# The third block solve of a chunked DeltaNet between the steps of its scan, and all gate blocks in the scan

## The chip, the cores and the metric

The kernel runs on one core of a Trainium2 chip. The metric is the device time of one execution in microseconds (us), from several runs of the same program; one more execution was recorded by the hardware profiler and is the source of every row below. The engines are TensorE (PE, its weight loads PEld), VectorE (DVE), ScalarE (ACT), GpSimd (POOL) and SP, whose queue issues nearly all DMAs.

## The reference, cut to what matters

One layer of a diffusion block over 512 latent tokens (and 256 context tokens that only feed the recurrent states), width 1024. Three mixers run on one input projection; their outputs are weighted by gates. This change touches the first mixer, a gated DeltaNet in chunks of 64 tokens, 8 heads of 128, in both directions, and the gates' projections.

```python
m = jnp.where(strict, jnp.einsum('bhnid,bhnjd->bhnij', kb, k) * decay, 0.0)
t_inv = lax.linalg.triangular_solve(eye + m, jnp.broadcast_to(eye, m.shape), left_side=True, lower=True)
u = jnp.einsum('bhnij,bhnjd->bhnid', t_inv, v * beta[..., None])
w = jnp.einsum('bhnij,bhnjd->bhnid', t_inv, kb * jnp.exp(gc)[..., None])
...
def step(state, inp):
    q_i, k_i, u_i, w_i, a_i, d_i = inp
    v_new = u_i - jnp.einsum('bhcd,bhde->bhce', w_i, state)
    o_i = jnp.einsum('bhcd,bhde->bhce', q_i, state) + jnp.einsum('bhcs,bhse->bhce', a_i, v_new)
    state = state * d_i[..., None, None] + jnp.einsum('bhcd,bhce->bhde', k_i, v_new)
    return state, o_i
...
o = rms_norm(o, norm_g) * jax.nn.silu(z)
...
g_dn, g_hy, g_lru = jnp.split(jax.nn.sigmoid(p_gate), N_BRANCH, axis=-1)
merged = g_dn * (o_dn @ w_proj_dn) + g_hy * (o_hy @ w_proj_hy) + g_lru * (o_lru @ w_proj_lru)
```

Each of the 12 chunks and 2 directions needs the inverse of a 64x64 unit triangular matrix per head before its step of the scan; the two directions run through the chunks in opposite order within the context (4 chunks) and the latent tokens (8 chunks).

## The kernel before, in words

All large products run in three passes on split weights and inputs (`mm3`: high x high, high x low, low x high). `load_w` loads a weight block of 512 KB into one of three raw buffers `wr`, splits it into one of two high (`wh`) and two low buffers (`wl`); the engines of the split are given per call (`e_hi`, `e_lo`). A gate block (`gate`, or `gate_halves` in two halves) is one `load_w`, 24 matmuls of 512 columns, one activation on ScalarE (L574) and one store to `gated` (L575). There are 24 such blocks beside the eight done early (`fill`: three kinds, eight each).

The inverses come from three solves (`solve`), two with four tiles of one direction each (`solve_first(0)`, `solve_first(1)`, on `M1`), and a third with the remaining two tiles of both directions (`solve_second`, on `M3`). A solve works on 32x32 blocks: transposes on VectorE bring the blocks' rows side by side (L819), 31 pairs of VectorE instructions eliminate column by column (L827, L829), transposes bring the inverse back (L837, L839), and TensorE makes the off-diagonal block from two chains of small products (L853, L857) with copies on ScalarE (L854, L858). The result is stored to `wad`, from where the scan loads it as `wa`. `solve` is a generator; `run` draws from the generators round by round and puts one piece of other work (`each`) behind every third round (`EVERY`). Before, 12 pieces (six values, six gates) lie beside the first two solves, and the remaining values and six gates beside the third (`NW1`, `NFILL`). A value (`value`, `value_out`) is a projection of 48 matmuls, a convolution of six VectorE instructions (L485 to L487), an activation and transposes.

The scan (`step`, L976 to L1041) has 12 steps. In each, both directions advance by a chunk: `chunk_loads` loads `v`, `kd` (three buffers each) and `wa` (ring `war`, four buffers); from step 1 on GpSimd scales the queries and keys by the decay (L992, L994); TensorE multiplies by the state (L1005); VectorE subtracts (L1009); TensorE applies the inverse (L1015); ScalarE copies the result (L1017). After the first `yield`, TensorE makes the state's increment (L1023), VectorE updates the state in 16 instructions (L1028; ScalarE instead in step 0, L1030), and in steps 4 to 11 TensorE finishes the output (L1035). Each step has two gaps, one at each `yield`; before, one half of a gate stands in each of the 24 gaps. Behind eight of the steps four `mod_part`s follow (a 512 KB load into a `wr` buffer and one VectorE instruction, L1052 or L1054), and before every third step a `mod_sum` (a few TensorE instructions into the bank of the gates).

Instructions are ordered per engine when the program is built: an instruction is placed when the scheduler's model has it ready, those written earlier first. In the scan, TensorE's order is fixed to the written one (`in_order((ET.PE,))`); the other engines' is not.

## Time and profile before

| | us |
|---|---|
| median of 3 runs | 1676.78 |
| lowest, highest | 1674.07, 1689.07 |
| profiled execution | 1676.85 |
| its span, first to last instruction | 1675.1 |
| TensorE busy | 1529.7 (91%) |
| VectorE busy | 1195.7 (71%) |
| ScalarE busy | 615.7 (37%) |
| GpSimd busy | 589.3 (35%) |

The busy times are from the page's first part. A matmul's recorded end is modelled, so matmuls overlap in the records and a busy TensorE need not be one at its peak; starts tell more than durations. The granted clock is a share of the upper level (2.4 GHz); at 0.5 it is the lower one. DVE, ACT and POOL instructions are recorded from start to end. SPq is SP's queue: what it "waited for" is what the next DMA in its order had to wait for.

### The profile page before, as it was taken

Reading aid. Unit: us, or ns where it says so; the run is one execution under the profiler, and the core shown is the slowest. Engines: PE = TensorE matmul, PEld = TensorE weight load, DVE = VectorE, ACT = ScalarE, POOL = GpSimd, SP = SyncE. Lnnn points to the kernel's source line nnn. Section 1 sums busy time; section 2 is a strip of 40 time slices with the busy share of each in tenths; the row PEclk is TensorE's granted clock in tenths of the full one; section 3 lists DMA queues with packets and bytes.
Section 4 is the critical chain, followed back from the end, with each engine's and each line's share of the span. In section 5 each row is a group of like instructions: output and inputs, shape, how many; then the busy total and the mean of one; then the engine's idle time right before and its main releaser. Section 6 shows DMA issues by size and latency. Waiting matters only on the chain. (4 is left out here: it accounts for less than half of the span.)

```text
span 1675.1 us, 23659 instructions
## 1 busy us (share of the span) xinstructions
PE 1529.7 (91%) x9176; PEld 1258.0 (75%) x9176; DVE 1195.7 (71%) x1752; ACT 615.7 (37%) x1011; POOL 589.3 (35%) x401
## 2 busy tenths in 40 slices
PE   6899888889999899887999889999999999999998
PEld 2677777767887777775788678787888788888876
DVE  6877888756656997834666375777766899989873
ACT  4367787734553232320111330333222433333311
POOL 4653534325444360312434114222321233334441
PEclk9899999999999896878899999999999999999999
DMA  9432222335344332577888736322462223232331
GB/s 343 162 107 82 76 76 81 103 104 175 127 126 125 110 101 74 173 211 206 233 227 244 253 109 231 107 88 84 162 207 64 68 96 97 92 101 98 104 113 50
DMA packets 93056, 225.66 MB, mean 135 GB/s; under 512 B 9963, under 2 KB 30699, under 8 KB 92176
## 3 DMA queue, kind: packets, MB, share of 16 engines
q1 hardware_dynamic: 92112, 217.86, 41.6%
q0 software_dynamic: 832, 6.29, 0.9%
q8 instruction: 72, 1.18, 0.3%
q14 instruction: 40, 0.33, 0.1%
HBM read 190.45 MB, written 33.66 MB: 134 GB/s over the span
## 5 line engine op out<-in xcount | busy, mean ns | idle before, releaser
L173 PE MATMUL bank<-region,region 128*128 128x512 f32 (+1 forms) x2032 | 761.8, 376 | 28.9 <-DVE region L487 6.8
L175 PE MATMUL bank<-region,region 128*128 128x512 f32 (+1 forms) x2032 | 755.2, 373 | 25.1 <-DVE region L160 22.1
L174 PE MATMUL bank<-region,region 128*128 128x512 f32 (+1 forms) x2032 | 757.2, 373 | 4.2 <-DVE region L160 2.1
L173 PEld LDWEIGHTS bank<-region,region 128*128 128x128 f32 x2032 | 389.7, 192 | 106.8 <-ACT region L155 10.4
L175 PEld LDWEIGHTS bank<-region,region 128*128 128x128 f32 x2032 | 389.5, 192 | 98.6 <-DVE region L160 28.6
L174 PEld LDWEIGHTS bank<-region,region 128*128 128x128 f32 x2032 | 390.6, 192 | 69.0 <-DVE region L418 4.4
L160 DVE TENSOR_TENSOR region<-region,region 128x1024 fp32r<-128x1024 f32 (+2 forms) x241 | 268.7, 1128 | 174.1 <-ACT region L155 98.2
L155 ACT ACTIVATE region<-region 128x1024 fp32r<-128x1024 f32 (+2 forms) x209 | 178.4, 865 | 422.9 <-PE bank L174 132.8
L160 POOL TENSOR_TENSOR region<-region,region 128x1024 fp32r<-128x1024 f32 (+1 forms) x64 | 157.3, 2463 | 237.9 <-ACT region L155 200.4
L157 POOL TENSOR_SCALAR region<-region 128x1024 fp32r<-128x1024 f32 (+1 forms) x96 | 114.3, 1193 | 330.4 <-PE bank L174 147.7
L1423 DVE SCALAR_TENSOR_TENSOR region<-bank,pc,region 128x441 f32<-128x441 f32 (+2 forms) x352 | 224.8, 688 | 4.3 <-ACT region L1412 0.7
L485 DVE SCALAR_TENSOR_TENSOR region<-bank,pc,region 128x511 f32<-128x511 f32 (+1 forms) x56 | 34.1, 629 | 48.7 <-ACT region L482 45.8
L1054 DVE SCALAR_TENSOR_TENSOR region<-region,cc,region 128x1024 f32<-128x1024 f32 x28 | 41.7, 1488 | 33.9 <-DMA region<-in_w_mod_dram 33.4
L992 POOL TENSOR_TENSOR region<-region,region 128x512 f32<-128x512 f32 x32 | 49.1, 1564 | 39.5 <-DMA region<-rowd 36.8
L482 ACT ACTIVATE region<-bank,pc 128x512 f32<-128x512 f32 (+1 forms) x40 | 23.1, 597 | 98.6 <-PE bank L175 98.6
L1435 POOL TENSOR_TENSOR region<-region,region 128x512 f32<-128x512 f32 x22 | 34.3, 1561 | 66.3 <-DVE region L1423 52.3
L1028 DVE SCALAR_TENSOR_TENSOR region<-region,egl,bank 128x128 f32<-128x128 f32 x160 | 42.3, 339 | 21.3 <-PE bank L1023 21.3
L1005 PE MATMUL bank<-region,region 128*64 128x128 f32 x608 | 42.4, 306 | 9.2 <-DVE region L1028 9.2
L1005 PEld LDWEIGHTS bank<-region,region 128*64 128x64 f32 x608 | 39.8, 157 | 14.4 <-DVE region L1028 6.4
L1017 ACT ACTIVATE region<-bank 128x512 f32<-128x512 f32 x24 | 14.3, 598 | 89.9 <-PE bank L1015 89.9
L574 ACT ACTIVATE region<-bank 128x512 f32<-128x512 f32 x32 | 18.8, 588 | 70.6 <-PE bank L175 66.4
L1137 POOL TENSOR_TENSOR region<-region,region 128x512 f32<-128x512 f32 x8 | 12.2, 1523 | 85.6 <-DVE region L1121 85.6
(275 smaller groups left out, 1669.7 us busy)
## 6 DMA issues: line engine op xcount, KB each, us to landing
region<-in_w_in_dram SPq DMA_DIRECT2D x97, 512.0 KB, 3.9
region<-in_w_mod_dram SPq DMA_DIRECT2D x48, 512.0 KB, 6.2
region<-in_ffn_up_dram SPq DMA_DIRECT2D x44, 512.0 KB, 3.5
region<-in_w_proj_dram SPq DMA_DIRECT2D x24, 512.0 KB, 3.6
region<-in_ffn_down_dram SPq DMA_DIRECT2D x22, 512.0 KB, 3.5
gated<-region SPq DMA_DIRECT2D x32, 256.0 KB, 2.1
region<-gated SPq DMA_DIRECT2D x32, 256.0 KB, 4.0
kdd<-region SPq DMA_DIRECT2D x16, 384.0 KB, 2.8
```

What stands on the lines that cost most here:

```text
L155: act(hi, raw, AF.Copy)
L157: nc.gpsimd.tensor_scalar(hi, raw, 1.0, 0.0, op0=ALU.mult, op1=ALU.add)
L160: (vtt if e_lo == "dve" else gtt)(lo, raw, hi.bitcast(F32), op=ALU.subtract)
L173: mmul(ps, lh, rh, start=start, stop=False)
L174: mmul(ps, lh, rl, start=False, stop=False)
L175: mmul(ps, ll, rh, start=False, stop=stop)
L992: gtt(wq[d][:, hs], KQ[hf][:, :, chs[d] - 4], eg[:, hs].unsqueeze(2).to_broadcast([P, 4, 2, 64]), op=ALU.mult)
L1005: mmul(X[hf][rcs[d], h, :], wq[d][:, hf * 4 + h, kind], S[d][:, hf * 4 + h, :], start=(kind == 0 or h == 0), stop=(kind == 0))
L1028: stt(S[d][:, h], S[d][:, h], egl[:, d, c, i, h:h + 1], p3[hf][d][:, h % 4], op0=ALU.mult, op1=ALU.add)
L1054: stt(acc, w_, cc[:, k, 0:1], acc, op0=ALU.mult, op1=ALU.add)
L1423: stt(uv[:, ro, co], pv_[:, ri, ci], w[:, a * 3 + b:a * 3 + b + 1], uv[:, ro, co], op0=ALU.mult, op1=ALU.add)
L1435: gtt(uu[0], uu[0], uu[1], op=ALU.mult)
```

## The change

The third solve leaves its own stage. Beside the first two solves lie the eight values alone (`NFILL = 0`), and no gate. All 24 gate blocks lie in the scan, 48 halves in 24 gaps, so two halves in each. `solve_second` is started ahead of the scan (`next(later)`: its opening transposes) and then advanced at every gap, four pieces in steps 0 to 3 and one from step 4 on; its block products get a `yield` between the forward and the back half. It uses buffers at 68, 72, 64 and 65 instead of 180 to 190, and banks 6 and 7. The scan's `wa` ring has two buffers in steps 0 to 6 (92 and 96) and four from step 7 on; `M3` (at 100) is in use until its store. Gate stores in the scan are issued by ScalarE's queue instead of SP's; `mod_sum` has bank 1 of its own. The six gates that were split on ScalarE and GpSimd (`"act", "pool"`) beside each solve now use the default engines, GpSimd for the high and VectorE for the low part.

```diff
--- before.py
+++ after.py
@@ -569,10 +569,10 @@
     def load_gate(z_, m, e_hi="pool", e_lo="dve"):
         return load_w(I["w_in"][GATES[z_][0] + m], e_hi=e_hi, e_lo=e_lo)
 
-    def gate_store(z_, m, pg):
+    def gate_store(z_, m, pg, store=load):
         th = ur([P, NL])
         act(th, pg, GATES[z_][1])
-        load(gated[z_, m], th)
+        store(gated[z_, m], th)
 
     def gate(z_, m, e_hi="pool", e_lo="dve"):
         w = load_gate(z_, m, e_hi, e_lo)
@@ -598,7 +598,7 @@
     ksr, knr, kdr = ring(3, [143, 140]), ring(3, seq(146, 3, 2)), ring(3, seq(152, 3, 2))
     qsr, jkr = ring(2, seq(140, 2, 5)), ring(0.5, seq(158, 0.5, 4))
     atr = ring(1, [170, 171])
-    NFILL = 12
+    NFILL = 0
 
     dcw = pv("dn_conv_w").rearrange("p (b j) -> p b j", j=4)
     kdd = dr.tile([2, TT, P, NH, P], F32, name="kdd")
@@ -843,15 +843,19 @@
         for half in range(2):
             zp = dn([P, 16, 32])
             rp = dn([P, 16, 32])
+            blocks = []
             for c in range(2):
                 d = dirs[c]
                 pj = slice(c * 64 + d * 32, c * 64 + d * 32 + 32)
                 pi = slice(c * 64 + (1 - d) * 32, c * 64 + (1 - d) * 32 + 32)
                 ci = slice((1 - d) * 32, (1 - d) * 32 + 32)
+                blocks.append((pj, pi, ci))
                 for a in range(16):
                     e = half * 16 + a
                     mmul(zp[pi, a, :], M[pj, e, ci], Wu[pj, e, :], start=True, stop=True)
                 act(Z[pi, half * 512:half * 512 + 512], zp[pi].rearrange("p a b -> p (a b)"), AF.Copy)
+            yield
+            for pj, pi, ci in blocks:
                 for a in range(16):
                     e = half * 16 + a
                     mmul(rp[pj, a, :], Z[pi, e * 32:e * 32 + 32], M[pi, e, ci], start=True, stop=True)
@@ -867,7 +871,7 @@
 
     def solve_second():
         yield from solve((0, 1), M3.rearrange("p t c h i -> p (t c h) i"),
-                         [at(180 + 4 * i, [P, 32, 32]) for i in range(2)], ring(1, seq(188, 1, 2)), "dve")
+                         [at(68 + 4 * i, [P, 32, 32]) for i in range(2)], ring(1, seq(64, 1, 2)), "dve")
         for d in range(2):
             for t, i in enumerate(second[d]):
                 load(wad[d, i, :, 0, :].rearrange("(c j) x -> j c x", c=2),
@@ -922,7 +926,7 @@
                 each.pop(0)()
 
     fill = [(z_, m) for z_ in range(3) for m in range(8)]
-    EVERY, NW1 = 3, 12
+    EVERY = 3
     vss = {}
 
     def values_(h):
@@ -933,10 +937,7 @@
 
     values = [lambda h=h: values_(h) for h in range(9)]
     ur = ring(2, [152, 154])
-    gates = [lambda f=f: gate(*f, "act", "pool") for f in fill[:NFILL]]
-    work = [w_ for p_ in zip(values, gates) for w_ in p_] + values[len(gates):] + gates[len(values):]
-    run([solve_first(0), solve_first(1)], work[:NW1])
-    run([solve_second()], work[NW1:])
+    run([solve_first(0), solve_first(1)], values + [lambda f=f: gate(*f, "act", "pool") for f in fill[:NFILL]])
     for nm, x_ in (("kdd", kdd), ("vd", vd), ("rowd", rowd)):
         dump(nm, x_)
     dump("egl", egl)
@@ -952,10 +953,11 @@
 
 
     ur = ring(2, [186, 188])
-    mm = Banks([0])
+    dn = Banks([6, 7])
+    mm, mm1 = Banks([0]), Banks([1])
     o = at(60, [P, 4, NH, P])
     S = [at(84 + 4 * d, [P, NH, P]) for d in range(2)]
-    war = ring(4, seq(92, 4, 4))
+    wars = [ring(4, [92, 96]), ring(4, [100, 104, 92, 96])]
     kdr, vr = ring(4, seq(140, 4, 3)), ring(4, seq(152, 4, 3))
     wqr = ring(4, seq(164, 4, 3))
     egr = ring(2, seq(176, 2, 2))
@@ -964,7 +966,7 @@
 
     def chunk_loads(s, lat):
 
-        v, kd, wa = vr([P, NH, P]), kdr([P, NH, P]), war([P, 2 if lat else 1, NH, 64])
+        v, kd, wa = vr([P, NH, P]), kdr([P, NH, P]), wars[s >= 7]([P, 2 if lat else 1, NH, 64])
         for d in range(2):
             i, c = divmod(order[d][s], 2)
             rc = slice(c * 64, c * 64 + 64)
@@ -1055,7 +1057,7 @@
 
     def mod_sum(q):
         if q in (1, 2):
-            mp = mm([P, 8])
+            mp = mm1([P, 8])
             for b in range(8):
                 mmul(mp[:, b:b + 1], acc[:, b * P:(b + 1) * P], ones[:, 0:1], start=True, stop=True)
             vtt(mod34[:, q - 1], mp, pv("b_mod")[:, 16 + q * 8:24 + q * 8], op=ALU.add)
@@ -1063,7 +1065,7 @@
             row, brow = wr([1, D]), wr([1, D])
             load(brow, I["b_mod"][:, (2 + q) * D:(3 + q) * D])
             for b in range(2):
-                mp = mm([1, 512])
+                mp = mm1([1, 512])
                 mmul(mp, ones[:, 0:1], acc[:, b * 512:(b + 1) * 512], start=True, stop=True)
                 vtt(row[:, b * 512:(b + 1) * 512], mp, brow[:, b * 512:(b + 1) * 512], op=ALU.add)
             load(modr[0 if q == 0 else 1].unsqueeze(0), row)
@@ -1073,10 +1075,12 @@
         project_part(w, [(pg, hh, hl)], 0, 4)
         yield
         project_part(w, [(pg, hh, hl)], 4, 8)
-        gate_store(z_, m, pg)
+        gate_store(z_, m, pg, nc.scalar.dma_start)
         yield
 
     first_ins = len(bb.instructions)
+    later = solve_second()
+    next(later)
     halves = (None for z_, m in fill[NFILL:] for _ in gate_halves(z_, m))
     ngap, FBM = 2 * (24 - NFILL), 1
     gap = 0
@@ -1088,9 +1092,11 @@
             gap += 1
             for _ in range(gap * ngap // 24 - (gap - 1) * ngap // 24):
                 next(halves)
+            for _ in range(4 if s_ < 4 else 1):
+                next(later, None)
         for k in range(4) if s_ % 3 < 2 else ():
             mod_part(s_ // 3, s_ % 3 * 4 + k)
-    assert next(halves, 1) == 1
+    assert next(halves, 1) == 1 and next(later, 1) == 1
     in_order((ET.PE,))
     dump("o", o)
     if upto <= 3:
```

## Rows read from the trace of the kernel before

**Rows 1.** Busy time by stretch; stretch: length, busy us per engine, granted clock, DMA share, GB/s
```profile
540.00:671.00 131.00, 117.40 (x956) 98.55 (x951) 116.29 (x221) 36.53 (x58) 43.23 (x13) 0.85 0.30 97
671.00:743.35 72.35, 60.98 (x484) 52.18 (x483) 43.18 (x57) 21.37 (x33) 21.14 (x14) 0.83 0.65 191
743.35:809.00 65.65, 52.76 (x452) 41.65 (x452) 34.80 (x62) 8.71 (x16) 14.79 (x13) 0.87 0.75 209
809.00:950.30 141.30, 132.77 (x1475) 112.61 (x1476) 82.07 (x174) 19.46 (x34) 51.97 (x37) 0.95 0.84 232
```

**Rows 2.** Timeline of TensorE: start, us, instruction, [idle before it and its releaser]
```profile
743.35 0.66 PE L1015 MATMUL bank<-region,region 64*64 64x128 f32 x2 [5.51 <-DMA region<-vd]
...
955.01 0.79 PE L173 MATMUL bank<-region,region 128*128 128x512 f32 x1 [4.24 <-ACT region L155]
```

**Rows 3.** SP's waits, 738 to 950 us: us in total, times, longest
```profile
SPq L575 <- ACT region L574: 35.1, 8, 9.0
```

**Rows 4.** Timeline of VectorE, first stage
```profile
592.21 1.12 DVE L485 SCALAR_TENSOR_TENSOR region<-bank,pc,region 128x511 f32<-128x511 f32 x2
...
595.36 1.79 DVE L827 TENSOR_TENSOR region<-region,region 128x256 f32<-128x256 f32 x1
...
647.63 1.88 DVE L839 STREAM_TRANSPOSE region<-region 32x1024 f32<-32x1024 f32 x1
```

**Rows 5.** Groups by line, 540 to 720 us: count, busy us, mean ns, idle before
```profile
L827 DVE TENSOR_TENSOR region<-region,region 128x31 f32<-128x31 f32 (+15 forms) x93 | 35.5, 406 | 1.1
L829 DVE TENSOR_TENSOR region<-region,region 128x31 f32<-128x31 f32 (+15 forms) x93 | 31.8, 365 | 1.1
L819 DVE STREAM_TRANSPOSE region<-region 32x1024 f32<-32x1024 f32 x12 | 25.5, 2121 | 0.3
L837 DVE STREAM_TRANSPOSE region<-region 32x1024 f32<-32x1024 f32 x12 | 25.4, 2118 | 0.3
...
L858 ACT ACTIVATE region<-bank 32x512 f32<-32x512 f32 x8 | 4.7, 588 | 18.8 <-PE bank L857 18.8
```

**Rows 6.** Timeline of all engines, from 683 us
```profile
683.07 2.39 POOL L160 TENSOR_TENSOR region<-region,region 128x1024 fp32r<-128x1024 f32 x1 [1.18 <-ACT region L155]
683.12 2.62 DVE L827 TENSOR_TENSOR region<-region,region 128x252 f32<-128x252 f32 x1
```

**Rows 7.** Timeline of TensorE, block products and gate matmuls
```profile
625.64 1.19 PE L853 MATMUL bank<-region,region 32*32 32x32 f32 x32 [1.16 <-DVE region L839]
...
691.18 0.40 PE L174 MATMUL bank<-region,region 128*128 128x512 f32 x1
...
695.95 0.39 PE L174 MATMUL bank<-region,region 128*128 128x512 f32 x1
```

**Rows 8.** DMA issues, 640 to 738 us: count, KB each, median us to landing
```profile
wad<-region SPq DMA_DIRECT2D x11, 256.0 KB, 2.9
...
region<-wad SPq DMA_DIRECT2D x4, 128.0 KB, 5.1
```

**Rows 9.** One line's instructions: count, ns min/median/max, first and last start
```profile
L575 SPq DMA_DIRECT2D gated<-region x32: 319/327/531, 125.5 to 955.5; - x32
```

**Rows 10.** Groups by line, 743 to 951 us
```profile
L1028 DVE SCALAR_TENSOR_TENSOR region<-region,egl,bank 128x128 f32<-128x128 f32 x160 | 42.3, 339 | 21.3 <-PE bank L1023 21.3
...
L1054 DVE SCALAR_TENSOR_TENSOR region<-region,cc,region 128x1024 f32<-128x1024 f32 x25 | 37.8, 1512 | 29.3 <-DMA region<-in_w_mod_dram 28.9
...
L1009 DVE TENSOR_TENSOR region<-region,bank 128x512 f32<-128x512 f32 x22 | 14.7, 681 | 5.8 <-PE bank L1005 5.8
...
L160 DVE TENSOR_TENSOR region<-region,region 128x1024 fp32r<-128x1024 f32 x10 | 13.8, 1378 | 23.5 <-POOL region L157 23.5
...
L157 POOL TENSOR_SCALAR region<-region 128x1024 fp32r<-128x1024 f32 x10 | 11.3, 1134 | 85.2 <-DMA region<-wad 30.3 <-PE bank L174 18.6 <-DMA region<-kdd 13.1
...
L994 POOL TENSOR_TENSOR region<-region,region 128x256 f32<-128x256 f32 x6 | 5.2, 887 | 14.5 <-PE bank L1005 14.3
```

**Rows 11.** DMA issues, 738 to 950 us
```profile
region<-kdd SPq DMA_DIRECT2D x20, 256.0 KB, 8.6
```

## The prediction

> **What bounds the kernel now.** I first cut the span with the busy-time-by-stretch view around the code that moves [rows 1]. The four stretches are the first two solves with their values and gates (540.00 to 671.00), the third solve with the last values and gates (to 743.35), the scan's steps 0 to 3 (to 809.00) and steps 4 to 11 (to 950.30). TensorE is the busiest engine in all four, yet never full: it lacks 13.6, 11.4, 12.9 and 8.5 us, and the granted clock is 0.85, 0.83, 0.87 and 0.95 of the upper level, so part of its busy time is stretched. VectorE has 116.3 of 131 us in the first stretch and 53 to 60% in the other three. So the first stretch is a VectorE stretch, steps 4 to 11 are a TensorE stretch, and the two in between are neither: something waits there. The timeline of TensorE shows what for: the scan's first matmul stood 5.51 us for the load of `vd`, and the first projection after the scan 4.24 us for a weight split on ScalarE [rows 2]. The list of waits on SP adds that SP, whose queue carries every load, stood 35.1 us in the scan at L575, the gate store, for ScalarE, once for 9.0 us [rows 3]; every load behind it starts later.
>
> **The change part by part.** I work on one clock, that of the profiled execution: 1675.1 us of span, 1676.85 us of time, 0.07 from the median 1676.78. A shift of the scan's end is taken as a shift of that time.
>
> *The first stage.* It keeps two solves and gets all eight values; six gates leave it. VectorE's last transpose of the first two solves begins at 647.63 and lasts 1.88, so it ends at 649.5 [rows 4]. What changes before that: the third solve's four opening transposes, done early, leave (4 x 2.121 = 8.5) [rows 5]. Two values come in, each with six convolution instructions: the solve is interrupted from 592.21 to 595.36 for one value [rows 4], so 6.3. And VectorE meets fewer splits on GpSimd. One such meeting reads: GpSimd's split starts at 683.07 and takes 2.39, the solve's instruction started at 683.12 takes 2.62 [rows 6], where the mean is 0.406 [rows 5]. Six gates less and two values more are four splits less, worth 0 to 4 x 2.2 = 8.8; I take 2, since most splits fall beside convolutions. The end moves to 649.5 - 8.5 + 6.3 - 2 = 645.3. TensorE has fewer matmuls here than now, so I cost them at nothing; VectorE covers them.
>
> *From there to the scan.* The last block products: two groups forward, two back, 1.19 each at the full clock [rows 7], with four copies of 0.588 [rows 5], 7.1; I take 8.5. Then SP stores (2.9 to landing) and loads `wad` (5.1) [rows 8], with two issues 8.9. The first scan matmul comes at 645.3 + 8.5 + 8.9 = 662.7 instead of 743.35: -80.7. Bounds: all of the 8.8 and 7.1 give 654.5; the products as slow as now (the stretch lasts until 671.0, 21.5 after VectorE's last transpose) and no relief give 677.7.
>
> *The gates in the scan.* A whole gate instead of a half stands in each of the 24 gaps. Starts of such matmuls lie 4.77 us apart over 21 of them, from 691.18 to 695.95 [rows 7], so 0.227 each and 2.73 for the twelve of a half: 8 x 2.73 = 21.8 in steps 0 to 3, 16 x 2.73 = 43.6 in steps 4 to 11. Its stores go from SP's queue to ScalarE's; an issue takes 0.33 [rows 9], 24 of them 8 us at the worst if each fell just ahead of a copy that the chain needs. I take nothing: a gate's copy is followed by the step's own matmuls before ScalarE has the next one, and ScalarE is 28.2 of 207 us busy [rows 1].
>
> The Trainium skill ("Trainium Kernel Development and Optimization", Key Constraints) says that issuing DMAs from several engines saves only the sequencer's issue time, as all share the same 16 DMA engines. By it the move is worth about 8 us of SP's time; the trace shows the 35.1 us of [rows 3] besides, which are not issue but an in-order queue held by a late producer.
>
> *Steps 0 to 3.* Two floors. TensorE: 52.76 busy [rows 1] + 21.8 = 74.6. VectorE, from 645.3 on: opening transposes 8.5; 31 pairs of solve instructions at 0.406 + 0.365, 23.9; six closing transposes at 2.118, 12.7 [rows 5]; 48 state updates at 0.339, 16.3; six subtractions at 0.681, 4.1; eight modulation parts at 1.512, 12.1; eight low splits at 1.378, 11.0 [rows 10]. That is 88.6, so it could be through at 733.9, 71.2 after the scan's start: much of the solve fits into step 0, where there is no state yet and VectorE has no update. Queued behind a solve instruction on VectorE are the step's subtraction and its 16 updates, for which TensorE waits; each is held by at most what stands before it. With floors of 74.6 and 71.2 and the present 12.9 us of waiting, half of which I leave (SP is freed of L575, but splits still wait for weights), steps 0 to 3 last 81 instead of 65.65: +15.4. Bounds: 74.6, and the 105.4 of the rival below.
>
> *Steps 4 to 11.* +43.6; the last half gate fills part of the 4.24 us wait [rows 2], -2.7; the third solve's products, eight groups at 1.19, +9.5, in gaps of steps 4 and 5, at TensorE's expense. The present 8.5 us of waiting shrink by 6, because a whole gate now stands between a step's products and the next step (a step's updates take 16 x 0.339 = 5.4) and the modulation sums no longer share the gates' bank. Sum +44.4, bounds +41.9 and +53. Two buffers of `wa` instead of four until step 6: I take nothing, as a load still has a whole step; the price otherwise is a rival. The four stores of the third solve are due two steps before step 8 reads them, with over 40 us for 2.9 + 5.1.
>
> Sum: -80.7 + 15.4 + 44.4 = -20.9, that is 1656.0. With every lower bound -88.9 + 9.0 + 41.9 = -38, 1639; with every upper one -65.7 + 39.8 + 53 = +27, 1704.
>
> **The rivals.** *TensorE is filled* (no waits in steps 0 to 3, the lower bounds): 1639. For it: SP's 35.1 us. Against: the splits of a gate now come twice as often while the modulation weights share their three raw buffers.
>
> *GpSimd blocks VectorE in steps 1 to 3.* GpSimd's 12 scalings at 0.887 and 8 high splits at 1.134 [rows 10] each hold VectorE for their length, as in [rows 6], 19.7; and half of the 28.9 us for which VectorE stood for modulation weights [rows 10] now falls on solve instructions queued behind, 14.5. Steps 0 to 3 then last 71.2 + 34.2 = 105.4, +39.8 instead of +15.4: 1676.85 - 80.7 + 39.8 + 44.4 = 1680. The means in my sum already hold some of this, which speaks against the full price. The Trainium skill ("SBUF — State Buffer", Who interferes with whom) states the mechanism as a rule: a VectorE instruction with two SBUF inputs and a GpSimd one that reads SBUF share a port, and the later one waits in full. [rows 6] agree; the rule speaks against bringing 62 such instructions beside GpSimd's work.
>
> *The solve runs in one block.* Its instructions depend only on each other, so the order fixed at compile time may place all of them ahead of step 1's subtraction, and the change does not interleave. 8.5 + 23.9 + 12.7 and four splits of 1.378 end at 695.9; step 1 wants VectorE two gates of 5.45 and three groups of matmuls after 662.7, some 17 us. That delays it by 16, half regained while VectorE is empty later: +8, 1664.
>
> *Slower: two `wa` buffers.* The load of step s waits at SP for step s - 2's last read, and behind it in order stand the loads of `kd` (8.6 us to landing) [rows 11], the decay rows and the gate weights. If steps 2 to 11 each wait for half of 8.6, that is 43: 1676.85 - 20.9 + 43 = 1699. It makes the kernel slower from 2.1 us a step on, by over 1% from 3.8. For it: SP has been late in this stretch already. Against: a step now takes about 20 us, more than twice the 8.6.
>
> **How the numbers follow.** Forecast 0.40 (its own range 1645 to 1672), filled 0.13, blocked by GpSimd 0.20, one block 0.10, `wa` 0.17. Within 1% (1660 to 1694) is what a measurement of this kernel can't tell from no change. Faster: 0.28 of the forecast, 0.13, 0.03 of the blocked, 0.04 of the block: 0.48. Slower: 0.15 of `wa` and 0.04 of the blocked, 0.19. Same: 0.33. The range 1634 to 1694 leaves out 0.03 below and 0.17 above; it holds cases of both signs.
>
> **What would show it.** The scan's first matmul near 663 (if after 678, the first stage is wrong); gates gone from the first stage and TensorE idle at its end; steps 0 to 3 near 81 us and steps 4 to 11 near 186; solve instructions on VectorE between the first matmul and step 4; no L575 in SP's waits. A line L972 or L973 in SP's waits of several us a step, with TensorE waiting for `wad` or `kdd`, would mean the `wa` rival; solve instructions of over 1 us beside GpSimd's, with TensorE waiting for L1009 or L1028, the blocked one. I am most unsure of steps 0 to 3, where two engines are nearly full and an in-order chain runs through both.

## The result

The changed kernel takes 1689.16 us (median of 15 runs) against 1678.69 (15 runs, the three of the table among them): ratio 1.0067, 95% interval 1.0051 to 1.0084. It is slower, by less than 1%; the forecast was 1656 and faster. The profiled execution took 1694.63 us, 17.8 above that of before, where the medians differ by 10.5: it is a slow one of its 15 runs, 5.5 above their median, and that of before lies 1.8 below its own. So some 7 of the 17.8 us are the scatter of single executions, and a stretch of one profile has its share of it.

Busy time by stretch, after; the cuts are 607.00 (TensorE's first long wait), 671.00 (the scan's first matmul came at 670.90), 760.71 (step 4's first) and 972.04 (the first projection after the scan):

```profile
core 0: us, PE busy (x) PEld busy (x) DVE busy (x) ACT busy (x) POOL busy (x), PEclk, DMA share, GB/s
540.00:607.00 67.00, 63.89 (x378) 55.39 (x377) 65.58 (x139) 21.97 (x37) 22.92 (x8) 0.97 0.36 109
607.00:671.00 64.00, 29.86 (x525) 28.18 (x524) 59.58 (x104) 12.59 (x23) 5.61 (x4) 0.52 0.48 136
671.00:760.71 89.71, 76.86 (x548) 60.61 (x548) 67.31 (x115) 11.03 (x19) 26.37 (x26) 0.89 0.71 199
760.71:972.04 211.33, 193.54 (x1925) 164.75 (x1924) 94.31 (x178) 36.14 (x80) 56.53 (x43) 0.93 0.70 202
sum 432.04, PE 364.15 PEld 308.93 DVE 286.78 ACT 81.72 POOL 111.43; mean PE 91.04 PEld 77.23 DVE 71.70 ACT 20.43 POOL 27.86
```

The same view of the kernel before, its stretch from 607.00 to 671.00 and the sum from 540.00 to 955.01, where its projection restarts:

```profile
607.00:671.00 64.00, 59.40 (x660) 49.70 (x660) 51.10 (x85) 19.77 (x32) 12.61 (x5) 0.77 0.27 89
...
sum 415.01, PE 364.39 PEld 305.04 DVE 277.59 ACT 89.59 POOL 131.13; mean PE 72.88 PEld 61.01 DVE 55.52 ACT 17.92 POOL 26.23
```

TensorE's busy time is the same, 364.15 and 364.39; its idle time grew from 50.6 to 67.9 us. By this account the loss is idle time. Equal busy sums don't say that the clock played no part: the matmuls that ran slower in steps 4 and 5 (4.5 us, below) must be made up for elsewhere. The idle time moved as well: 34.1 us of it now lie in the second stretch, ahead of the scan, at a granted clock of 0.52; before, the same 64 us had 59.4 busy at 0.77, with the gates in them. The gates now stand in the scan, which TensorE ends.

TensorE's timeline after, at the places that matter (start, duration, engine, line, operands; in brackets the wait before it):

```profile
661.28 1.91 PE L861 MATMUL bank<-region,region 32*32 32x32 f32 x32 [0.68 <-ACT region L862]
...
670.90 4.32 PE L1017 MATMUL bank<-region,region 64*64 64x128 f32 x32 [7.72 <-issue]
...
698.50 1.11 PE L1017 MATMUL bank<-region,region 64*64 64x128 f32 x7 [6.97 <-DVE region L1011]
...
760.71 3.71 PE L1007 MATMUL bank<-region,region 128*64 128x128 f32 x64
...
772.76 1.19 PE L855 MATMUL bank<-region,region 32*32 32x32 f32 x32
774.70 1.19 PE L855 MATMUL bank<-region,region 32*32 32x32 f32 x32 [0.74 <-ACT region L856]
776.57 3.60 PE L1025 MATMUL bank<-region,region 64*128 64x128 f32 x32 [0.68 <-ACT region L856]
...
787.66 1.19 PE L861 MATMUL bank<-region,region 32*32 32x32 f32 x32
789.53 1.55 PE L861 MATMUL bank<-region,region 32*32 32x32 f32 x32 [0.68 <-ACT region L862]
791.01 3.57 PE L1062 MATMUL bank<-ones,region 128*128 128x1 f32 x16
794.52 6.53 PE L1007 MATMUL bank<-region,region 128*64 128x128 f32 x64
...
903.73 3.68 PE L1017 MATMUL bank<-region,region 64*64 64x128 f32 x32 [5.63 <-DVE region L1011]
```

A chain of the block products is 16 matmuls; the rows count 32, as each of these f32 matmuls leaves two records. Three things are to be seen. The first solves' last products (L861 is the old L857) take 1.91 us a chain where [rows 7] had 1.19; the 7.72 behind them are the store and the load of `wad`. Step 1 stands 6.97 us for a subtraction on VectorE, the wait of 903.73 is of the same kind. And each piece of the third solve's products, two chains, holds a wait of 0.7 for ScalarE's copy between them; the two forward pieces have a second one ahead of L1025. L1025 writes banks 6 and 7 too, so the products have no banks of their own, nor has `mod_sum` bank 1, which the same increments use. Three of the four pieces are followed by matmuls at a lower clock (granted 0.85 from 776.57 to 787.66, 0.73 from 791.01 to 808.54 and from 825.27 to 836.00; 1.00 behind the third): the modulation sum took 3.57 us (L1062, the old L1060), in the kernel before 1.95, and the products with the state behind it 6.53 (L1007) where step 4's own took 3.71.

### The profile page after: what moved, and what is told of

Same layout as the page of the kernel before. It is cut to its first block, busy times and chain, and to the rows that moved or that the text cites. A ratio compares the mean times of both kernels' runs of the same rounds, so it can differ in the third digit from the quotient of the medians.

```text
span 1692.7 us, 23658 instructions
## 1 busy us (share of the span) xinstructions
PE 1530.3 (90%) x9176; PEld 1264.5 (75%) x9176; DVE 1203.5 (71%) x1764; ACT 604.7 (36%) x999; POOL 566.5 (33%) x401
## 5 line engine op out<-in xcount | busy, mean ns | idle before, releaser
L160 DVE TENSOR_TENSOR region<-region,region 128x1024 fp32r<-128x1024 f32 (+2 forms) x253 | 286.9, 1146 | 213.2 <-POOL region L157 113.4
L155 ACT ACTIVATE region<-region 128x1024 fp32r<-128x1024 f32 (+2 forms) x197 | 165.7, 853 | 408.1 <-PE bank L174 126.3
L157 POOL TENSOR_SCALAR region<-region 128x1024 fp32r<-128x1024 f32 (+1 forms) x108 | 134.4, 1246 | 375.1 <-PE bank L174 221.1
L160 POOL TENSOR_TENSOR region<-region,region 128x1024 fp32r<-128x1024 f32 (+1 forms) x52 | 117.7, 2269 | 194.7 <-ACT region L155 157.4
L994 POOL TENSOR_TENSOR region<-region,region 128x512 f32<-128x512 f32 x32 | 46.5, 1477 | 57.3 <-DMA region<-rowd 29.6
L485 DVE SCALAR_TENSOR_TENSOR region<-bank,pc,region 128x511 f32<-128x511 f32 (+1 forms) x56 | 34.1, 631 | 31.8 <-ACT region L482 29.0
L1441 POOL TENSOR_TENSOR region<-region,region 128x512 f32<-128x512 f32 x22 | 34.4, 1562 | 66.8 <-DVE region L1429 60.0
L1017 PE MATMUL bank<-region,region 64*64 64x128 f32 x384 | 29.1, 307 | 24.3 <-DVE region L1011 16.6
L1019 ACT ACTIVATE region<-bank 128x512 f32<-128x512 f32 x24 | 14.3, 597 | 93.1 <-PE bank L1017 84.8
L1017 PEld LDWEIGHTS bank<-region,region 64*64 64x64 f32 x384 | 25.4, 154 | 27.1 <-DVE region L1011 18.3
L1007 PEld LDWEIGHTS bank<-region,region 128*64 128x64 f32 x608 | 39.4, 156 | 4.8 <-issue 4.3
```

Of the source, the lines that this page charges most:

```text
L155: act(hi, raw, AF.Copy)
L157: nc.gpsimd.tensor_scalar(hi, raw, 1.0, 0.0, op0=ALU.mult, op1=ALU.add)
L160: (vtt if e_lo == "dve" else gtt)(lo, raw, hi.bitcast(F32), op=ALU.subtract)
L994: gtt(wq[d][:, hs], KQ[hf][:, :, chs[d] - 4], eg[:, hs].unsqueeze(2).to_broadcast([P, 4, 2, 64]), op=ALU.mult)
L1007: mmul(X[hf][rcs[d], h, :], wq[d][:, hf * 4 + h, kind], S[d][:, hf * 4 + h, :], start=(kind == 0 or h == 0), stop=(kind == 0))
L1017: mmul(W[hf][rc, h, :], wa[rc, 0, hf * 4 + h, :], rhs, start=True, stop=True)
```

## The experiments

Stretches are compared from the scan's first matmul on, since single executions differ by up to 7 us in code that no edit touches (the last of the early query copies came between 437.9 and 445.6 us). "First stage" is what lies ahead of that matmul, and a step begins with its first matmul. Each ratio is against runs of the kernel before that were made beside it (their medians lie between 1676.2 and 1681.5), so ratios compare kernels better than medians do.

### Each move alone

The gates alone: the third solve keeps a stage ahead of the scan.

```diff
-    run([solve_first(0), solve_first(1)], values + [...])
+    run([solve_first(0), solve_first(1)], values)
+    run([solve_second()], [])
...
-    later = solve_second()
-    next(later)
+    later = iter(())
```

> The changed kernel with the third solve kept in a stage of its own ahead of the scan (nothing beside it), all 24 gates in the scan. Theory 'paid twice': the gates are the loss, since they leave a stretch that VectorE ends and enter one that TensorE ends. First scan matmul near 705 (solve 37 after the second one's end at 650, products and wad 18), -38; steps 0 to 3 about 88 (+22), steps 4 to 11 about 186 (+45): about 1700 us. Theory 'the solve breaks the scan': without solve instructions between the steps they last near their floors, 78 and 176, so about 1685 us or less.

Measured 1684.87 us, ratio 1.0040 (1.0012 to 1.0068). The scan's first step could start at 675.68, ahead of the third solve's products, but step 1 came at 723.39. Steps 4 to 11, from step 4's first matmul to step 11's, took 155.4 instead of 125.3: +30.1 where 14 half gates at 2.73 are 38.2. So the gates alone cost steps 4 to 11 no more than forecast. Steps 0 to 3 took 111.6: the third solve's products, which end at 713.8, stand between step 0 and step 1. The time is that of the second theory, these stretches are not.

The solve alone: twelve gates back in the first stage, in turn with the values as before.

```diff
-    NFILL = 0
+    NFILL = 12
...
+    work = [w_ for p_ in zip(values, gates) for w_ in p_] + values[len(gates):] + gates[len(values):]
+    run([solve_first(0), solve_first(1)], work)
```

> The changed kernel with twelve gates in the first stage as before the change (half a gate in each gap of the scan), the third solve between the steps. Theory 'paid twice': the first stage is now ended by TensorE at about 715 (-25), steps 0 to 3 cost +10, steps 4 to 11 +15: about 1676 us, like the kernel before. Theory 'the solve breaks the scan': steps 0 to 3 +16, steps 4 to 11 +25, about 1692 us.

1693.71 us, 1.0104 (1.0053 to 1.0155; four runs): slower than before, and not clear of the changed kernel's 1.0067. Steps 4 to 11 took 141.3 (+16.0), and ahead of the scan nothing was gained. TensorE's timeline shows why:

```profile
743.44 0.66 PE L1019 MATMUL bank<-region,region 64*64 64x128 f32 x2 [21.40 <-DMA region<-vd]
```

The first scan matmul stood 21.4 us for `vd` and came when it had come before, at 743.4. Neither move pays alone, and neither theory holds whole in this run or the one above.

### What ends the first stage

All nine value steps ahead of the gates (`work = values + gates`), else as the solve alone:

> Twelve gates in the first stage as in the solve-only kernel, but all nine value steps ahead of them (there value and gate alternated, and the scan's first matmul stood 21.4 us for the load of vd). If that late value was the whole reason why the solve alone gained nothing ahead of the scan: the first scan matmul comes 21 earlier, at about 722, and the time is about 1672 us. If TensorE's projections end the stage anyway: 735 or later, 1686 us.

1680.08 us, 1.0030 (1.0006 to 1.0053). The first scan matmul came at 734.13 and still waited 12.70 for `vd`. So neither expectation holds: the late value was part of it only. Next, the gates' results of the first stage in other buffers, since those lie in the scan's first `v` buffer:

```diff
-    ur = ring(2, [152, 154])
+    ur = ring(2, [186, 188])
```

> As the kernel with twelve gates in the first stage and the values ahead of them, with the first stage's gate results in other buffers (at 186 and 188 instead of 152 and 154, where the scan's v buffers lie). There the scan's first matmul stood 12.7 us for vd. If the load of v waited for the buffers of the last gates: that wait goes, the first scan matmul comes near 722, about 1668 us, faster than before. If the load is late by its place in SP's queue: the wait stays, 1680 us.

1672.10 us, 0.9961 (0.9939 to 0.9984). No wait is left: the matmul of 717.20 follows the last gate directly. A buffer shared between two stages had held the load of `v`. Against the changed kernel the scan's first matmul comes 46.3 later and the scan to step 11 is 67 shorter (209.2 instead of 276.2): the twelve gates, 65 us of matmuls by the prediction's price, cost the first stage 46. The same two edits in the kernel before (results at 190 and 192):

> The kernel before with the same two edits: values ahead of the gates, the gate results of the first stage at 190 and 192. The solve stays in the first stage. If the first stage of the kernel before was ended by its late values and the shared buffers rather than by the third solve: its 5.5 us wait for vd goes and the third solve is no longer held up by the last three values, first scan matmul at about 730 instead of 743, about 1665 us, faster than before and than the changed kernel. If the third solve and TensorE's projections end it together: 738 to 743, 1672 to 1677 us.

1678.24 us, 1.0000 (0.9971 to 1.0029). The first stage did become shorter (step 1 at 743.7 instead of 755.2), but steps 4 to 11 took 144.2 instead of 125.3; TensorE waited 18.2 us, ten times, for GpSimd's scaling L992. Why it comes later there was not tried.

Six gates in the first stage, a piece of other work at every second round (`NFILL = 6`, `EVERY = 2`):

> As the one with twelve gates in the first stage, but six of them there, a value or gate at every second piece of the two solves instead of every third. Theory 'paid twice': six gates (33 us of TensorE) just fill the 21 us that TensorE stood in the first stage and keep its clock up, so the first scan matmul comes near 675 (-68), and six gates less in the scan take about 33 off its 300: about 1665 us, faster than both. Theory 'the solve breaks the scan': the scan keeps its waits, 1680 us.

1682.62 us, 1.0031 (1.0007 to 1.0054). The first matmul came at 692.8, 18 later than hoped, with values again at the end; the scan to step 11 took 250.9 instead of 276.2.

### The third solve's products

Left out (the third solve's `mmul` chains into `zp` and `rp` and their copies under `if dirs[0] == dirs[1]:`):

> The changed kernel without the third solve's block products and their four copies (its inverse blocks stay uncombined); the products of the first two solves stay. In the trace they take 14.3 us in the gaps of steps 4 and 5, and the granted clock is 0.5 to 0.7 after each of the four pieces. If the products cost only their stretches: 14 less, 1675 us. If the clock falls because of them: 22 to 28 less, 1663 us, with the gates of steps 5 and 6 at 2.7 instead of 3.7 to 6.5 us a half. If the queues of VectorE and SP set steps 4 to 11: under 8 less.

1667.94 us, 0.9953 (0.9929 to 0.9977): 1.14% less than the change, some 19 us. In the profiles steps 4 to 11 took 161.4 instead of 186.4, but only 19.7 of these 25 us lie in steps 4 and 5, where the products stand. The rest lies in steps 6 to 10, where the profile of the change took 121.8 and this one 116.6; a kernel with the products in the same places (the one with other raw buffers, below) took 115.3 there. So the products cost about 20 us, not the 9.5 of the forecast and not the 14.3 that they occupy. Then they stay, in eight groups, one behind each half gate (a `yield` behind the first chain of each piece makes the groups):

```diff
                 next(halves)
+                if s_ >= 4:
+                    next(later, None)
-            for _ in range(4 if s_ < 4 else 1):
+            for _ in range(4 if s_ < 4 else 0):
                 next(later, None)
```

> The changed kernel with the third solve's products cut into eight groups of 16, one behind each half gate of steps 4 and 5, instead of four pieces of 32. Theory 'clock': small matmuls in a row let the granted clock fall, and the eight waits of 0.7 for the copies stand between them; spread among the wide matmuls both go: 10 to 14 of the 25 us that leaving them out gave come back, 1676 us. Rival 'work': the products cost their matmuls wherever they stand: 1686 to 1690 us.

1681.99 us, 1.0026 (1.0005 to 1.0047), 0.4% less than the change; steps 4 to 11 took 173.5 in the profile, which is of the fastest of its ten runs. Steps 4 and 5, by stretch (columns as above), of the changed kernel, of the spread and of the one without products:

```profile
760.71:825.27 64.56, 59.66 (x689) 52.50 (x688) 23.15 (x48) 13.16 (x21) 16.98 (x13) 0.89 0.70 190
```
```profile
757.88:814.69 56.81, 55.14 (x689) 47.15 (x689) 23.91 (x48) 13.18 (x21) 17.06 (x13) 0.97 0.77 215
```
```profile
760.83:805.68 44.85, 43.37 (x433) 37.22 (x432) 21.02 (x45) 9.05 (x14) 15.99 (x13) 1.00 0.91 243
```

The first 75 us from step 4 on, in the same order:

```profile
760.71:836.00 75.29, 70.39 (x795) 62.48 (x795) 28.78 (x52) 14.95 (x24) 22.23 (x16) 0.86 0.71 191
```
```profile
757.88:833.00 75.12, 73.45 (x887) 63.03 (x887) 36.21 (x70) 16.76 (x27) 24.07 (x18) 0.98 0.78 219
```
```profile
760.83:836.00 75.17, 68.17 (x707) 58.56 (x708) 39.87 (x73) 12.63 (x20) 30.04 (x22) 0.99 0.92 249
```

With all products done, the spread kernel has a granted clock of 0.98 there against 0.86, and 1.7 us of idle against 4.9. In steps 4 and 5 the same 689 matmul records take 4.5 us less of TensorE's time (59.66 and 55.14), and 3.2 us of idle go. So of the 19.7 us, 7.8 (64.56 - 56.81) are the clock and the copies' waits, and 12.0 (56.81 - 44.85) remain with the products between the gates. The times agree: 0.41% and 0.73%, 7 and 12 us, each give or take 5. Both theories have a part, and the rival's is the larger.

### Steps 0 to 3

The third solve left out altogether (`later` only makes the four stores to `wad`):

> The changed kernel without the third solve (its triangular blocks go to wad as they are, so the scan's last third works on wrong inverses): beside the kernel without its products alone it leaves out VectorE's 31 pairs and ten transposes too. Theory 'the solve's block holds step 1': steps 0 to 3, from the first scan matmul to step 4's first, fall from 90 to about 82, and the time is about 1660 us, 8 below the kernel without the products. Rival 'the gates' weights and the modulation loads hold steps 0 to 3': they stay at 88 or more and the time at 1667 us.

1661.17 us, 0.9914 (0.9883 to 0.9944). Steps 0 to 3 took 83.7; the other kernels with all gates and the third solve in the scan took 88.5 to 92.7 there (89.8 after), but for the one below with VectorE's order fixed. The solve costs them about 6 in the profiles; without it TensorE is busy 74.6 us of these steps, the floor of the forecast, and idle 9.1:

```profile
676.53:760.27 83.74, 74.60 (x548) 59.42 (x548) 36.92 (x72) 11.05 (x19) 22.87 (x22) 0.93 0.74 211
```

But step 1 still waited 4.91 us; VectorE's timeline of this kernel shows for what:

```profile
687.86 1.23 DVE L160 TENSOR_TENSOR region<-region,region 128x1024 fp32r<-128x1024 f32 x1 [10.50 <-POOL region L157]
697.53 1.53 DVE L1056 SCALAR_TENSOR_TENSOR region<-region,cc,region 128x1024 f32<-128x1024 f32 x1 [8.44 <-DMA region<-in_w_mod_dram]
698.98 1.21 DVE L160 TENSOR_TENSOR region<-region,region 128x1024 fp32r<-128x1024 f32 x1
700.12 1.27 DVE L1011 TENSOR_TENSOR region<-region,bank 128x512 f32<-128x512 f32 x2
```

The subtraction L1011 is queued behind a modulation part that waits 8.44 us for its load. In the changed kernel the same place holds the solve as well:

```profile
691.83 1.90 DVE L837 STREAM_TRANSPOSE region<-region 32x1024 f32<-32x1024 f32 x1
693.59 1.20 DVE L1056 SCALAR_TENSOR_TENSOR region<-region,cc,region 128x1024 f32<-128x1024 f32 x1
694.73 2.01 DVE L839 STREAM_TRANSPOSE region<-region 32x1024 f32<-32x1024 f32 x1
696.65 1.20 DVE L160 TENSOR_TENSOR region<-region,region 128x1024 fp32r<-128x1024 f32 x1
697.78 1.27 DVE L1011 TENSOR_TENSOR region<-region,bank 128x512 f32<-128x512 f32 x2
```

Two causes stand one behind the other, and taking one away leaves part of the other. VectorE held to the written order (`in_order((ET.PE, ET.DVE))`):

> The changed kernel with VectorE's instructions in the scan held to the order in which the code writes them, four pieces of the third solve behind each half step. In the changed kernel VectorE runs the solve nearly in one block, 655 to 709, and step 1's first subtraction stands 7 us behind it. Theory 'one block': step 1's wait of 7 goes and steps 0 to 3 last about 82 instead of 90: 1681 us. Rival 'VectorE is simply full there': the same work ends later, steps 1 to 3 wait in smaller portions, and the modulation parts that wait for their loads now hold the chain: 1690 us or slower.

1732.03 us, 1.0332 (1.0285 to 1.0379). It is no test of the block, since it pins the weight splits too (TensorE stood 26.6 us for L160); step 1's wait did not go (9.5 us for L1011). It shows what the scheduler's order is worth. Other raw buffers for the modulation weights from step 4 on (`ring(4, [76, 80])`):

> The changed kernel with two raw buffers of their own for the modulation weights from step 4 on, so that the gates have all three of theirs. Theory 'shared buffers': VectorE's 38.4 us of waits for w_mod and the chain behind them (5.63 of TensorE at 903, 2.25 at 877, 2.75 at 963) go, steps 4 to 11 shorter by 8 to 12: 1679 us. Rival: those waits are hidden but for the one at 903: 0 to 4 less, 1686 us.

1687.55 us, 1.0060 (1.0040 to 1.0081): within the interval of the change. VectorE's waits for those loads, from the scan's first matmul on, fell from 35.1 to 10.8 us and those for GpSimd's half of the split rose from 64.8 to 88.5; the wait moved. The scan's gate weights split on ScalarE and GpSimd (`load_gate(z_, m, "act", "pool")`):

> The changed kernel with the scan's gate weights split on ScalarE (high part) and GpSimd (low part) instead of GpSimd and VectorE. It takes 24 low splits of 1.3 us and their waits for GpSimd (64.8 us in the scan) out of VectorE's queue, ahead of the state updates and subtractions. Theory 'VectorE's queue sets the steps': TensorE's 16.6 us of waits for the subtraction shrink to under 6: 1679 us. Rival 'GpSimd's two-input split holds VectorE as long as the split itself took, and ScalarE's copy stands in front of the chain's copies': no gain, 1689 us or slower.

1694.58 us, 1.0108 (1.0076 to 1.0139). TensorE's wait for the subtraction is 16.6 us as in the changed kernel. Taking the low splits out of VectorE's queue freed nothing there.

### The edits costed at nothing

In the kernel before, two `wa` buffers and the gate store on ScalarE's queue:

```diff
-    war = ring(4, seq(92, 4, 4))
+    wars = [ring(4, [92, 96]), ring(4, [100, 104, 92, 96])]
...
-        gate_store(z_, m, pg)
+        gate_store(z_, m, pg, nc.scalar.dma_start)
```

> The kernel before with two of the change's small edits and nothing else: two wa buffers instead of four until step 6, and the scan's gate stores on ScalarE's queue. The prediction put both at nothing. Theory 'nothing': 1677 us, within 0.3% of before. Rival 'two wa buffers': 20 us and more slower, with TensorE waiting for wad or kdd. Rival 'SP was late': the 35.1 us at the gate store were worth something, 4 to 10 us faster.

1684.60 us, 1.0043 (1.0020 to 1.0066). The scan to step 11 took 193.1, in the kernel before 193.4; TensorE waited for neither `wad` nor `kdd`. SP did stand at the load of `wa` for the earlier step's matmuls, 10.9 us in four waits, but the scan is no longer for it: the two buffers cost it nothing. Where the 0.4% lie this profile doesn't show. The store alone:

> The kernel before with the scan's gate stores on ScalarE's queue and nothing else. With two wa buffers beside it the kernel before took 1684.6 us, although its scan was as long as before's (193.1 us from the first matmul to step 11) and its profile was already 5 us late 300 us ahead of any edit. Theory 'that offset is none of the edits'': 1677 us, within 0.3%. Rival 'the two wa buffers cost it': 1677 us or less here, too, but then by the scan's stretch. Rival 'the store on ScalarE costs it': 1684 us again.

1691.30 us, 1.0089 (1.0055 to 1.0124). SP's list of waits over the scan begins with

```profile
SPq L1050 <- DMA region<-in_w_mod_dram: 22.9, 6, 8.3
SPq L1227 <- PE bank L1067: 16.2, 1, 16.2
```

so the 35.1 us of [rows 3] are gone, and the scan to step 11 is not shorter: 205.4. The Trainium skill ("Trainium Kernel Development and Optimization", Key Constraints) has it that issuing DMAs from several engines saves only issue time; these two runs of the kernel before agree in that no time came of the 35.1 us. That the store alone costs more than with two `wa` buffers beside it is not explained. In the changed kernel, the store back on SP (`gate_store(z_, m, pg)`):

> The changed kernel with the scan's gate stores back on SP's queue. Alone, their move to ScalarE's queue made the kernel before 0.9% slower, although SP's 35 us at the gate store went with it. If ScalarE's queue is the worse place: 1680 us or less here, with ScalarE's 8.3 us of waits for the store gone. If a late SP is the worse one when all gates lie in the scan (24 stores instead of 12): 1695 us or more, SP standing over 60 us at the gate store. If it makes no difference: 1689 us.

1698.22 us, 1.0117 (1.0078 to 1.0157). SP stood 45.6 us at the store, and steps 4 and 5 took 72.8 instead of 64.6; with all 24 stores in the scan its queue looks the worse place, by four runs whose interval just meets that of the change.

### A version faster than both

The kernel with 0.9961, its products in groups ahead of and behind the half gate of a gap:

```diff
+            if s_ >= 4:
+                next(later, None)
             for _ in range(gap * ngap // 24 - (gap - 1) * ngap // 24):
                 next(halves)
```

> The fastest kernel so far (twelve gates in the first stage behind the values, their results in buffers of their own, the third solve between the steps; 1672 us) with the third solve's products in eight groups, one ahead of and one behind the half gate of a gap. Theory 'clock and copies': as spreading them gave 0.4% in the changed kernel, about 1666 us. Rival 'with half a gate in a gap there are too few wide matmuls between the groups to keep the clock': 1672 us.

1666.53 us, 0.9930 (0.9909 to 0.9952). Steps 4 and 5 took 44.6 instead of 50.7, at a granted clock of 1.00 instead of 0.90. Then eight gates in the first stage:

> The same with eight gates in the first stage instead of twelve. If the scan has waits that four more gates fill (24 us of waits for VectorE in it): the first scan matmul 20 earlier, at about 697, the scan 12 to 15 longer, 1661 us. If each gate costs the scan its full 5.5 us: 1667 us, as with twelve.

1673.00 us, 0.9963 (0.9934 to 0.9992), slower than both expectations: the scan to step 11 took 30.6 longer, and its first matmul came 18 earlier (counted from VectorE's first Gram product, 511.1 in the one and 505.6 in the other). Four gates cost the scan more than they free ahead of it. At last the twelve stores on SP's queue:

> The fastest kernel so far (twelve gates in the first stage behind the values, their results in buffers of their own, the third solve between the steps, its products in eight groups; 1666.5 us) with the scan's twelve gate stores back on SP's queue as in the kernel before. If ScalarE's queue is the worse place: 1655 to 1660 us. If SP's lateness costs as much: 1666 us, within 0.3%.

1658.64 us, 0.9875 (0.9842 to 0.9909; four runs), the fastest. Its stretches, cut at its own first scan matmul, step 4 and restart:

```profile
540.00:607.00 67.00, 64.08 (x379) 55.87 (x378) 65.57 (x142) 24.10 (x41) 23.02 (x9) 0.97 0.36 108
607.00:671.00 64.00, 55.50 (x589) 44.34 (x589) 62.30 (x102) 17.35 (x27) 15.33 (x5) 0.72 0.45 128
671.00:716.63 45.63, 45.63 (x216) 37.55 (x213) 21.57 (x33) 11.98 (x15) 19.63 (x13) 0.94 0.66 196
716.63:783.58 66.95, 50.71 (x453) 40.19 (x453) 41.11 (x74) 9.75 (x17) 16.10 (x14) 0.90 0.79 221
783.58:937.95 154.37, 141.94 (x1732) 120.02 (x1732) 80.39 (x168) 27.22 (x55) 43.79 (x37) 0.96 0.83 227
sum 397.95, PE 357.86 PEld 297.97 DVE 270.95 ACT 90.41 POOL 117.87; mean PE 71.57 PEld 59.59 DVE 54.19 ACT 18.08 POOL 23.57
```

TensorE is without a gap from 671 to the scan, and its idle time is 40.1 us, against 50.6 and 67.9. Its scan to step 11 is as long as that of the version before it (203.0 and 203.1), so where the last 0.5% come from these profiles don't show, and the two intervals meet.

## Why the prediction was wrong

Sum by the profile: -72.45 + 24.2 + 65.3 = +17.1, where the prediction had -80.7 + 15.4 + 44.4 = -20.9. (Steps 0 to 3 from 670.90 to 760.71 against the 65.65 of [rows 1], steps 4 to 11 and the restart 211.3 against 146.0. The 809.00 of [rows 1] is the end of step 3's last gate; step 4's first matmul came at 811.46, behind a wait that this cut gives to steps 4 to 11. After the change the two marks are one.) By its steps:

- *First stage*, 645.3 forecast for VectorE's last transpose, 650.2 measured; 1.9 of it was there ahead of the region. So the end moved by -1.2 where -4.2 was forecast: the direction right, 3.0 short.
- *From there to the scan*, 17.4 forecast, 20.7 measured. The step that failed is "two groups forward, two back, 1.19 each at the full clock": six groups stand behind that transpose, at the lower clock, 1.91 each, 13.0 with three waits for copies where 8.5 was taken; the store and the load took 7.7 instead of 8.9. The trace of before had both, 1.19 at 625.64 and 1.91 at 653.10, just as VectorE's transposes end; the prediction kept the slow one as its bound and took the other. With the first stage 8.3 us missing.
- *Gates in the scan* at 2.73 a half: right. Without the products, steps 4 to 11 up to step 11's first matmul took 161.4, against 127.8 before from 809.00 on: +33.6; 14 halves at 2.73 less the 6 us of waits are 32.2.
- *Steps 0 to 3*, 81 forecast, 89.8 measured. The failed step is that half of "the present 12.9 us of waiting" was taken off: TensorE stood 12.9 us there after the change as well, and was busy 77.0 where the floor was 74.6. The prediction put the solve at nothing beyond VectorE's floor; it is worth 6 of the 8.8, as step 1 met VectorE's queue. Without it 9.1 us of waiting are left, 2.7 more than forecast. SP's freedom, which was to take the waiting away, gave nothing in the kernel before.
- *Steps 4 to 11*, +44.4 forecast, +65.3 measured. The mis-sized term is the third solve's products: 9.5 forecast, 19.7 measured in steps 4 and 5, 10.2 of the 20.9. 12.0 of the 19.7 is what the products cost between wide matmuls; the rest is the clock behind the pieces and the copies' waits, of which the sum had nothing. 5.2 more are steps 6 to 10 of this one profile, which the medians don't bear out. 3.9 more lie between step 11's first matmul and the restart (18.3 before, 24.9 after, where +2.8 was forecast), where a gate waited 2.75 for its weights.
- *The edits at nothing*: right for the two `wa` buffers, whose rival fell. For the store, see above: the times have a price in the kernel before and, less surely, a gain in the changed one, and neither is explained.

Of the rivals, "one block" was the nearest for steps 0 to 3: VectorE ran the solve from 655 to 709 with one wait of 3.3, and step 1 stood 7 us. "Blocked by GpSimd" shows in single solve instructions of 0.8 to 1.2 us, but the solve ended at 709, inside step 1, where that rival had it hold steps 1 to 3. None of the rivals held the clock, and the slower side was given to a mechanism that cost TensorE nothing.

These terms make up the miss. Why there was so little to gain stood in the sum, as 65.4 us of gates in the scan against 2 off the first stage, and was not asked about: a stretch that VectorE ends is free room for TensorE's gates, and the change gave the room up. With twelve gates back there the kernel went from 1.0067 to 0.9961. The fastest version keeps both, the solve in the scan and twelve gates in the first stage.

## What to carry to other kernels

Before moving work out of a stretch because another engine ends it, count the idle time of TensorE over all stretches together: here 364 us of work stayed and 17 us of idle came. Chains of small matmuls with copies between them are priced with the granted clock that follows them, and here did better between wide ones, group by group. A profile is one execution: before a stretch is priced by the difference of two, see whether the medians give as much. Where a stage starts late for a load, look whose buffers it loads into.

## What the runs showed of the hardware

- 16 small matmuls (32x32) took 1.19 us at a granted clock of 1.00 (the kernel before at 625.64) and 1.91 at 0.50 (at 653.10). From 650 to 670 us of that kernel TensorE has no gap in its records, over half of its time in such chains and the rest in wide matmuls between them, and the granted clock is 0.50.
- Over the 75 us from step 4 on, with four pieces of 32 of them, the granted clock was 0.86, with the same products in eight groups between wide matmuls 0.98, without them 0.99.
- The modulation sum (8 matmuls of one column, 16 records) took 3.57 us right behind such a piece, 1.84 to 1.95 elsewhere.
